# One level of Strassen's scheme for the up projection of a gated MLP, over pairs of a gate tile and a value tile, with the activations kept in DRAM

## Chip, cores, metric

One core of a Trainium2 chip runs one decoder layer. The metric is the device time of one execution in microseconds (us), from several runs; lower is better. PE is the tensor engine, DVE the vector engine, ACT the scalar engine, POOL is GpSimd, and SP is the engine that issues most DMAs.

## The reference

A decoder layer on 1024 tokens of width 1024 in float32: a Mamba-2 SSD branch and a latent attention branch, merged by gates and projected (`w_o`), then a gated MLP with a causal convolution over three tokens. Only the end is touched by the change:

```python
x = x + (g_ssd * y_ssd + g_mla * y_mla) @ w_o[i]
h = rms_norm(x, norm_ffn_g[i])
u = causal_depthwise_conv(h @ w_up[i], conv_ffn_w[i], conv_ffn_b[i])   # 1024 -> 2 * 2816
u_gate, u_val = jnp.split(u, 2, axis=-1)
x = x + (jax.nn.silu(u_gate) * u_val) @ w_down[i]                      # 2816 -> 1024
```

## The kernel before

Every large product is made of float32 numbers split in two: a rounded high part (type fp32r) and the rest. `split` (L126) makes the high part by a cast on ACT (L127) and the low part by a subtraction on DVE or POOL (L128). `mm3` (L147) multiplies two such numbers in three matmuls (L149 high by high, L150, L151 the cross terms), so one step over 128 input channels, for 128 output channels and 512 tokens, is three matmuls of 128x512.

The program is written in the order of the work. PE keeps the order in which the code is written. A scheduler may shift instructions on the other engines, each of which then takes its own in order; SP issues DMAs in order too, and one that has to wait holds up those behind it.

The stages at the end, with their places in the span: the SSD projection and merge for the two token halves, the output projection `w_o`, in the page's names `wops`, the norm (L208 to L229), transposition of the normed tokens to channels (`transposed`, L235 to L238), then the up projection and the down projection. `h2[half][k]` are the eight transposed and split tiles of a token half, in the pool `hp` (name `h`). The up projection goes over 22 gate tiles (kind 0) and 22 value tiles (kind 1) of 128 channels. For each it loads and splits the weight tile (`load_w`, names `wraw`, `whi`, `wlo`; the low part on DVE here), does eight steps of `mm3` for each half, and evacuates:

```python
ps = lin_tile()
yield from steps([w], h2[half], ps, range(KD), KD)
a = half * 512
S.copy(raw[:, 2 + a:2 + a + 512], ps)
c = act[:, a:a + 512] if kind == 0 else lt.tile([P, 512], F32, name="lt")
S.activation(c, ps, AF.Identity, bias=col(CG_FB + ct), scale=col(cw + 2))
for k in range(2):
    V.scalar_tensor_tensor(c, raw[:, a + k:a + k + 512], col(cw + k), c, op0=ALU.mult, op1=ALU.add)
if kind == 0:
    S.activation(c, c, AF.Silu)
else:
    V.tensor_tensor(act[:, a:a + 512], act[:, a:a + 512], c, op=ALU.mult)
```

The 22 tiles `act` (128 channels by 1024 tokens) stay in SBUF. The down projection goes over two halves of the output columns (`ch`) and 11 pairs of channel tiles (`kp`); it splits `act` again for each `ch` and accumulates into eight PSUM banks (six `dps`, two `lin`).

Of the kernel before, what the change touches and what calls it, by code (L numbers as in the profile page):

```python
# [9 lines left out]
F32 = mybir.dt.float32  # L10
# [7 lines left out]
P = 128  # L18
# [12 lines left out]
# column offsets of the packed per-partition parameters  # L31
# [19 lines left out]
# shape-only constants kept on chip; the rope tables and the attention mask follow them  # L51
# [5 lines left out]
# linear steps laid between the steps of the dependent chains, one digit for each place  # L57
# [15 lines left out]
def tile_hybrid_layer(ctx: ExitStack, tc: tile.TileContext, x, cols, cons, w_main, w_small, w_uq, w_ukv,  # L73
# [39 lines left out]
    def rsqrt_mean(dst, ss, n):  # L113
        # the halved exponent as a first guess, three Newton steps
# [32 lines left out]
    def mm3(ps, a, b, first, last):  # L147
        (ah, al), (bh, bl) = a, b
        PE.matmul(ps, lhsT=ah, rhs=bh, start=first, stop=False)  # L149
        PE.matmul(ps, lhsT=ah, rhs=bl, start=False, stop=False)  # L150
        PE.matmul(ps, lhsT=al, rhs=bh, start=False, stop=last)  # L151
# [25 lines left out]
    # linears that fill the tensor engine between the steps of the dependent chains  # L177
# [24 lines left out]
    def norm(tiles, outs, pool, ss=None, junk=None, group=1):  # L202
        """token-major rms norm; yields where other work may come in between"""
# [48 lines left out]
    # ---------------------------------------------------------------- linears of the hidden state that can wait  # L252
# [32 lines left out]
    # ---------------------------------------------------------------- norm, transposed hidden, token-major projection  # L285
# [44 lines left out]
        # the tensor engine's clock rises with its use: transposes of the identity until the data are there  # L330
# [43 lines left out]
    # q_a / kv_a norms and transposes  # L374
# [27 lines left out]
    # rope tables with the gains: [cos g1, sin g2, sin g1, cos g2]  # L402
# [7 lines left out]
    # shared rotary key part: sum of squares, rotated with gains  # L410
# [12 lines left out]
    # dt = softplus(raw + bias) = max(v, 0) + log1p(exp(-|v|)); log1p(e) = 2 atanh(e / (2 + e))  # L423
# [18 lines left out]
    # a = dt * -exp(a_log), its cumulative sums per chunk, the decays  # L442
# [15 lines left out]
    # the convolved channels come doubled: dt / 2 for x, dt / 8 for x, B and the C that reads the state  # L458
# [13 lines left out]
    # ---------------------------------------------------------------- attention  # L472
    with tc.tile_pool(name="cp", bufs=2) as cp, tc.tile_pool(name="pss", bufs=4, space=PSUM) as pss, \
# [3 lines left out]
        # the same mask with the keys on the partitions, and the negated identity  # L477
# [4 lines left out]
        # the columns of maxima stand last behind others, so that their row comes out in the place of the last channel  # L482
# [6 lines left out]
        def qkv_steps(pr):  # L489
            """q, k, v of a pair of heads, token-major, a half of the tokens at a time, with the norms and the rope"""  # L490
# [7 lines left out]
            for half in range(2):  # L498
                # a last channel: 0 of q, for the row of maxima, and 1 of k
# [64 lines left out]
        def maxima(pr, half, hd):  # L564
            """the greatest product of the high parts for each query of a half, negated, as a last row of q"""
# [28 lines left out]
        def key_block(pr, half, j, hd, accs):  # L594
            """exponentials of the scores of a key block for the queries of a half, transposed; their sums over blocks"""
# [24 lines left out]
        def output(pr, half, accs, pv):  # L620
            """values not yet normalized, and the sums as rows"""
# [30 lines left out]
        # the side steps of the units: done before the first key block, then after each step of the key blocks  # L652
        SIDE = [[1, 1, 1, 1, 1, 1, 1, 1, 2, 2, 2, 2], [1] * 10 + [0] * 1 + [2] * 7 + [0] * 6]

        def attention():
            """per unit (pair, half of the queries): key blocks one by one, the values two behind; the maxima of the
            next unit and the projection of the next pair go in between"""
# [14 lines left out]
            for pr in range(npair):  # L672
                for half in range(2):
# [13 lines left out]
                    # the first half's keys are overwritten only after their last use  # L687
# [28 lines left out]
    # ---------------------------------------------------------------- SSD, one group of eight heads at a time  # L716
    ya0 = [None] * 16
    head = []
    with tc.tile_pool(name="dp", bufs=2) as dp, tc.tile_pool(name="psx", bufs=1, space=PSUM) as psx, \
# [46 lines left out]
            # masked scores, transposed, with the decays  # L766
# [73 lines left out]
        def ssd_finish(g):  # L840
            # gate with silu(z) (kept doubled), then the group's norm
# [47 lines left out]
        def normalize(k):  # L889
            """attention output of two heads over its sums"""  # L890
# [61 lines left out]
    # ---------------------------------------------------------------- SSD branch projection, merge, output projection  # L952
    uctx = ExitStack()
    up = uctx.enter_context(tc.tile_pool(name="up", bufs=2))
    with tc.tile_pool(name="ep", bufs=2) as ep, tc.tile_pool(name="psw", bufs=4, space=PSUM) as psw, \
            tc.tile_pool(name="eps", bufs=2, space=PSUM) as eps_:
        x2h = []
        h2 = [[], []]
        for half in range(2):
            s = hs_(half)  # L960
            ya = ya0 if half == 0 else [load_act(y_d, k * P, s) for k in range(16)]
            ms = []
            for ct in range(8):
                gt = ep.tile([P, 512], F32, name="gt")
                nc.scalar.dma_start(out=gt, in_=g_d[ct * P:(ct + 1) * P, s])
                mt = ep.tile([P, 512], F32, name="mt")
                nc.scalar.dma_start(out=mt, in_=m_d[ct * P:(ct + 1) * P, s])
                if half == 0 and ct == 0:
                    ps = head[0]
                else:  # L970
                    ps = lin_tile()
                    drain([steps([load_w(w_ssd[ct, kp], [P, KD, P]) for kp in range(2)], ya, ps, range(16), 16)])
                V.scalar_tensor_tensor(gt, gt, 1.0, ps, op0=ALU.add, op1=ALU.mult)
                V.tensor_tensor(gt, gt, mt, op=ALU.add)
                m = ep.tile([P, 2, 512], F32R, name="m", bufs=8)
                S.mul(m[:, 0, :], gt, 0.5)
                V.scalar_tensor_tensor(m[:, 1, :], gt, 0.5, m[:, 0, :].bitcast(F32), op0=ALU.mult, op1=ALU.subtract)
                ms.append(m)
            if half:
                drain([norm(x2h[0], x2h[0], ep, x2ss)])  # L980
            x2s = []
            for i in range(4):
                t_ = ep.tile([P, D], F32, name="x2", bufs=8)
                r0 = (half * 4 + i) * P
                nc.sync.dma_start(out=t_, in_=x[r0:r0 + P, :])
                x2s.append(t_)
            x2h.append(x2s)
            sq4 = ep.tile([P, 4, 4], F32, name="sq4")
            for cq in range(4):
                banks = [psw.tile([P, 512], F32, name="wops") for _ in range(4)]  # L990
                qs = slice(cq * 256, (cq + 1) * 256)
                for kp in range(2):
# [179 lines left out]
```

## Time and profile before

| | us |
|---|---|
| runs | 2411.93, 2413.11, 2416.68 |
| median | 2413.11 |
| span of the profiled execution, first to last instruction | 2408.0 |
| PE busy in the span | 2277.5 (95%) |
| DVE, ACT, POOL busy | 1338.8, 1015.2, 489.5 |
| up projection, in the span | about 1684 to 2164.4 |
| down projection | 2164.4 to 2404 |

The profile gives the profiled execution its span and no time of its own; the median of the runs is 5.1 us over that span, which is what lies around it. Matmuls overlap in the pipe, so a matmul's duration in the profile (389 ns for 128x512) is not what it costs in a row of them; that is the distance between starts. In the whole up and down projection POOL does 44 small memsets and nothing else.

### The profile page before, as it was taken

The page shows a single profiled execution, that of the slowest core. Times are in us where ns is not written, and L with a number is a line of the kernel's source. Part 1 is how long each engine was busy: PE and PEld are TensorE (multiplying, and loading weights), DVE is VectorE, ACT ScalarE, POOL GpSimd, SP SyncE. Part 2 cuts the span into 40 slices and gives each one's busy share as a digit, 9 for nine tenths or more (in the row PEclk, how much of TensorE's full clock was granted, in tenths as well). Part 3 has the DMA queues.
Part 4 walks back from the last instruction along what each step waited for, and adds up shares of the span by engine and source line. Part 5 has one row for each costly group of instructions (what it writes and reads, how often), then busy time and mean ns, then how long its engine had stood idle before and what let it go on. Part 6 is the DMA issues. An engine that isn't in the chain of part 4 may idle for free.

```text
span 2408.0 us, 31951 instructions
## 1 busy us (share of the span) xinstructions
PE 2277.5 (95%) x11752; PEld 1833.4 (76%) x11752; DVE 1338.8 (56%) x2614; ACT 1015.2 (42%) x2020; POOL 489.5 (20%) x643
## 2 busy tenths in 40 slices
PE   8999999999999979988889699999999999999999
PEld 7877777777777757767667578989888888888887
DVE  4566666567644766767755555545544444453332
ACT  4454545444434364463643423424433333342221
POOL 2244443334423423232333300000000000000000
PEclk9999999999999989999999899999999999999999
DMA  3111111111126532243436466543111111111312
GB/s 134 54 63 59 50 46 36 59 50 50 40 69 183 158 90 76 91 108 91 90 124 221 145 225 203 171 149 116 61 44 53 44 53 44 53 44 61 104 63 87
DMA packets 139004, 220.57 MB, mean 92 GB/s; under 512 B 12544, under 2 KB 49088, under 8 KB 138848
## 3 DMA queue, kind: packets, MB, share of 16 engines
q1 hardware_dynamic: 133808, 208.97, 28.3%
q10 hardware_dynamic: 5040, 9.57, 1.1%
q8 instruction: 92, 1.51, 0.3%
q14 instruction: 64, 0.52, 0.1%
HBM read 173.14 MB, written 45.35 MB: 91 GB/s over the span
## 4 chain that ended last, share of the span: by engine, by line
PE 48%; DMA 9%; DVE 5%; ACT 3%; issue 3%; POOL 1%; SPq 0%; POOLq 0%; DVEq 0%; ACTq 0%
PE lin L149 11%; PE lin L150 11%; PE lin L151 11%; DMA abc<-ac_d 5%; PE dps L150 2%; PE dps L151 2%; PE dps L149 2%; DVE chan L740 2%; PE wops L151 1%; PE wops L150 1%; PE wops L149 1%; DMA zt<-z_d 1%; ACT seg L771 1%; PE yp L812 1%; DVE seg L774 1%
## 5 line engine op out<-in xcount | busy, mean ns | idle before, releaser
L149 PE MATMUL lin<-h,whi 128*128 128x512 f32 x1984 | 806.8, 407 | 29.3 <-ACT chan L738 19.1
L150 PE MATMUL lin<-h,whi 128*128 128x512 f32 x1984 | 782.1, 394 | 3.2 <-DVE h L128 3.2
L151 PE MATMUL lin<-h,wlo 128*128 128x512 f32 x1984 | 780.9, 394 | 2.1 <-DVE wlo L128 2.0
L149 PEld LDWEIGHTS lin<-h,whi 128*128 128x128 f32 x1984 | 378.3, 191 | 155.2 <-issue 54.4
L151 PEld LDWEIGHTS lin<-h,wlo 128*128 128x128 f32 x1984 | 377.2, 190 | 85.2 <-DVE wlo L128 2.9
L150 PEld LDWEIGHTS lin<-h,whi 128*128 128x128 f32 x1984 | 378.9, 191 | 72.6 <-DVE h L128 4.7
L127 ACT CAST whi<-wraw 128x512 fp32r<-128x512 f32 x372 | 223.9, 617 | 370.2 <-PE lin L150 151.7
L128 DVE TENSOR_TENSOR wlo<-wraw,whi 128x512 fp32r<-128x512 f32 x234 | 160.0, 695 | 221.5 <-ACT whi L127 218.7
L128 POOL TENSOR_TENSOR wlo<-wraw,whi 128x512 fp32r<-128x512 f32 x138 | 195.4, 1429 | 311.4 <-ACT whi L127 301.9
L606 ACT ACTIVATE e<-s 128x512 f32<-128x512 f32 (+1 forms) x192 | 93.4, 492 | 160.2 <-DVE s L604 109.4
L740 DVE SCALAR_TENSOR_TENSOR chan<-craw,cl,chan 128x512 f32<-128x512 f32 x144 | 143.8, 999 | 26.8 <-ACT chan L738 17.0
L1024 POOL MEMSET uraw<- 128x2 f32 x44 | 4.3, 100 | 746.0 <-DVE act L1036 495.9
L771 ACT ACTIVATE seg<-abc,acum 128x128 f32<-128x128 f32 x256 | 80.0, 389 | 134.9 <-DMA abc<-ac_d 125.0
L611 POOL TENSOR_TENSOR acc<-acc,e 128x512 f32<-128x512 f32 (+3 forms) x80 | 79.1, 989 | 222.6 <-ACT acc L609 134.4
L128 DVE TENSOR_TENSOR h<-act,h 128x1024 fp32r<-128x1024 f32 x44 | 53.1, 1224 | 104.2 <-ACT h L127 104.2
L1036 DVE SCALAR_TENSOR_TENSOR lt<-uraw,cl,lt 128x512 f32<-128x512 f32 x88 | 66.0, 750 | 75.3 <-ACT lt L1034 74.6
L149 PE MATMUL dps<-whi,h 128*128 128x512 f32 x264 | 102.7, 389 | 0.0
L150 PE MATMUL dps<-wlo,h 128*128 128x512 f32 x264 | 102.7, 389 | 0.0
L151 PE MATMUL dps<-whi,h 128*128 128x512 f32 x264 | 102.7, 389 | 0.0
L1036 DVE SCALAR_TENSOR_TENSOR act<-uraw,cl,act 128x512 f32<-128x512 f32 x88 | 66.0, 750 | 63.9 <-ACT act L1034 63.1
L127 ACT CAST h<-act 128x1024 fp32r<-128x1024 f32 x44 | 45.6, 1048 | 119.0 <-PE lin L150 112.9
L1032 ACT COPY uraw<-lin 128x512 f32<-128x512 f32 x88 | 51.5, 586 | 100.1 <-PE lin L151 100.0
(414 smaller groups left out, 3825.5 us busy)
## 6 DMA issues: line engine op xcount, KB each, us to landing
wraw<-in_w_main SPq DMA_DIRECT2D x112, 256.0 KB
wraw<-in_w_up SPq DMA_DIRECT2D x88, 256.0 KB
abc<-ac_d SPq DMA_DIRECT2D x32, 512.0 KB
wraw<-in_w_ssd SPq DMA_DIRECT2D x64, 256.0 KB
wraw<-in_w_down SPq DMA_DIRECT2D x44, 256.0 KB
g_d<-lt SPq DMA_DIRECT2D x32, 256.0 KB
z_d<-lt SPq DMA_DIRECT2D x32, 256.0 KB
zt<-z_d SPq DMA_DIRECT2D x32, 256.0 KB
```

Of the source, the lines that this page charges most:

```text
L127: S.copy(hi, raw)
L128: (eng or V).tensor_sub(lo, raw, hi.bitcast(F32))
L149: PE.matmul(ps, lhsT=ah, rhs=bh, start=first, stop=False)
L150: PE.matmul(ps, lhsT=ah, rhs=bl, start=False, stop=False)
L151: PE.matmul(ps, lhsT=al, rhs=bh, start=False, stop=last)
L606: S.activation(e[:, c0:512], ps[:, 0:w], AF.Exp)
L611: (V if hd else G).tensor_tensor(accs[hd][:, c0:512], accs[hd][:, c0:512], e[:, c0:512], op=ALU.add)
L740: V.scalar_tensor_tensor(c[:, s], raw[:, a + k:a + k + 512], col(cw + k), c[:, s], op0=ALU.mult, op1=ALU.add)
L771: S.activation(seg[:, hd, :], abc[:, hd, :], AF.Relu, bias=acum[:, c, 8 * g + hd:8 * g + hd + 1], scale=-1.0)
L774: V.tensor_tensor(seg, seg, sm.unsqueeze(1).broadcast_to([P, 8, P]), op=ALU.mult)
L1032: S.copy(raw[:, 2 + a:2 + a + 512], ps)
L1036: V.scalar_tensor_tensor(c, raw[:, a + k:a + k + 512], col(cw + k), c, op0=ALU.mult, op1=ALU.add)
```

## The change

The up projection of one gate tile and one value tile is taken as a product of a 2 by 2 matrix of weight blocks (rows: gate, value; columns: the two halves of the 1024 input channels) with a 2 by 2 matrix of activation blocks (rows: halves of the input channels; columns: token halves). It is computed with seven block products in place of eight, in the variant with shared sums. A block product is four steps of `mm3`.

- Activations: the seven blocks `11`, `21`, `22`, `t1` to `t4` (28 tiles `BQ[name][i]` of 128x512, split in two) are made once at the entry of the MLP from the transposed tiles. `h2_raw` transposes and scales without a split; DVE (L1192, L1203, L1210) and POOL (L1201) make the differences; `quarter` (L988 cast on ACT, L989 subtraction on DVE or POOL) splits.
- Weights: per pair `w_raw` loads the gate tile to `ur1` and the value tile to `ur2`, whole; `w_sums` makes sums and differences in four POOL instructions (L1100 to L1103); `w_first` to `w_fourth` split four sets (casts L1091, subtractions L1092; the first two sets on POOL, the others on DVE).
- The seven products are `p12` (two), `p5`, `p6`, `p7`, `p3`, `p4`; some accumulate onto an earlier one in its PSUM bank after that has been read. PSUM is read by ACT copies (L1134, L1144) and DVE additions (L1135, L1146, L1153, L1166, L1172) that put the parts together to `ug` and `uv` (1024 tokens). The convolution, SiLU and product then run on 1024 tokens at once (L1159 to L1174).
- The product is written to the DRAM tensor `a_d`; the down projection reads it back as `ar`, once for each `ch`.
- `x2_d` is written in pieces of 256 columns during `w_o`; all PSUM outside `lin` is one pool of six banks (`bank6`). The rows read at the end of the down projection have places of their own (`xr`).

The comments were also taken out of the code. The core of the diff:

```diff
+        def w_sums(q):
+            q.s = up.tile([P, KD, P], F32, name="us", bufs=1)
+            G.tensor_tensor(q.s[:, 0:4, :], q.r2[:, 0:4, :], q.r2[:, 4:8, :], op=ALU.add)
+            G.tensor_tensor(q.s[:, 4:8, :], q.s[:, 0:4, :], q.r1[:, 0:4, :], op=ALU.subtract)
+            G.tensor_tensor(q.r2[:, 0:4, :], q.r1[:, 0:4, :], q.r2[:, 0:4, :], op=ALU.subtract)
+            G.tensor_tensor(q.r1[:, 4:8, :], q.r1[:, 4:8, :], q.s[:, 4:8, :], op=ALU.subtract)
+        def w_second(q):
+            q.b = w_split(q.s, w_tiles(1), G)
+        def w_third(q):
+            q.c = w_split(q.r2, w_tiles(2), V)
...
+        def p5(q):
+            q.z = bank6()
+            drain([product(q.z, q.b, 0, "t1", True, True)])
+        def p6(q):
+            drain([product(q.x, q.b, 4, "t2", False, True)])
+            q.s2 = lt.tile([P, 512], F32, name="lt")
+            S.copy(q.s2, q.x)
+            q.q = lt.tile([P, 512], F32, name="lt")
+            V.tensor_tensor(q.q, q.z, q.s2, op=ALU.add)
+        def p7(q):
+            q.y = bank6()
+            drain([product(q.y, q.c, 0, "t3", True, True)])
...
+            V.tensor_tensor(q.uv[:, 514:1026], q.y, q.q, op=ALU.add)
...
+        def p3(q):
+            drain([product(q.z, q.d, 0, "22", False, True)])
+            V.tensor_tensor(q.ug[:, 514:1026], q.z, q.s2, op=ALU.add)
+            q.gate = conv(q, 0, q.ug)
+            S.activation(q.gate, q.gate, AF.Silu)
+        def p4(q):
+            drain([product(q.y, q.c, 4, "t4", False, True)])
+            V.tensor_tensor(q.uv[:, 2:514], q.y, q.s2, op=ALU.add)
+            c = conv(q, 1, q.uv)
+            V.tensor_tensor(q.gate, q.gate, c, op=ALU.mult)
+            nc.sync.dma_start(out=a_d[q.j * P:(q.j + 1) * P, :], in_=q.gate)
...
-        for j in range(2, FFT):
-            for kind in range(2):
-                drain([up_half(j, kind, 0), up_half(j, kind, 1)])
...
+    for j in range(3, FFT + 1):
+        nx = None
+        if j < FFT:
+            nx = Pair()
+            nx.j = j
+            w_raw(nx)
+            w_first(nx)
+            gate_row(nx)
+        p5(q)
+        if nx:
+            w_sums(nx)
+        p6(q)
+        if nx:
+            w_second(nx)
+        p7(q)
+        p3(q)
+        if nx:
+            w_fourth(nx)
+        p4(q)
+        if nx:
+            w_third(nx)
+            drain([p12(nx)])
+            c11(nx)
+        q = nx
...
+                    ar = fp.tile([P, T], F32, name="ar")
+                    nc.sync.dma_start(out=ar, in_=a_d[k * P:(k + 1) * P, :])
                     hi = hp.tile([P, T], F32R, name="h")
                     lo = hp.tile([P, T], F32R, name="h")
-                    split(acts[k], hi, lo)
+                    split(ar, hi, lo)
```

How instructions stand on the engines, at three places. In the names, a number after the last underscore is the buffer. First POOL, from the end of the SSD stage: before, the sums of squares of the last group's norm are followed by the memsets of the up projection alone.

```order
L858 TENSOR_TENSOR sqs<-sqs,sq__12696 128x512
L858 TENSOR_TENSOR sqs<-sqs,sq__12702 128x512
L858 TENSOR_TENSOR sqs<-sqs,sq__12708 128x512
L1024 MEMSET uraw 128x2 x44
```

Now, at the entry of the MLP, POOL splits pair 0's second set (`wlo_15698`), makes pair 1's sums and splits its second set, and does the quarters of the activations (`tq`, `h`) and the differences L1201, one after the other:

```order
L1092 TENSOR_TENSOR wlo_15698<-us_15692,whi_15697 128x1024
L1100 TENSOR_TENSOR us_15773<-ur2_15572 128x512
L1101 TENSOR_TENSOR us_15773<-us_15773,ur1_15571 128x512
L1102 TENSOR_TENSOR ur2_15572<-ur1_15571,ur2_15572 128x512
L1103 TENSOR_TENSOR ur1_15571<-ur1_15571,us_15773 128x512
L989 TENSOR_TENSOR tq_15660<-x2_13592,tq_15660 128x512
L1092 TENSOR_TENSOR wlo_15779<-us_15773,whi_15778 128x1024
L989 TENSOR_TENSOR tq_15689<-x2_13592,tq_15689 128x512
```

Four L1201 and six more L989 follow; the fifth of these six is the last that `p6` of pair 0 needs. Second, DVE in the middle of the up projection. Before, per weight tile (value tile, then the next gate tile):

```order
L1036 SCALAR_TENSOR_TENSOR lt_17220<-uraw_17182,cl_80,lt_17220 128x512 x2
L1040 TENSOR_TENSOR act_17109<-act_17109,lt_17220 128x512
L128 TENSOR_TENSOR wlo_17332<-wraw_17333,whi_17331 128x512
L1036 SCALAR_TENSOR_TENSOR lt_17251<-uraw_17182,cl_80,lt_17251 128x512
L128 TENSOR_TENSOR wlo_17332<-wraw_17337,whi_17331 128x512
L1036 SCALAR_TENSOR_TENSOR lt_17251<-uraw_17182,cl_80,lt_17251 128x512
```

Now, per pair:

```order
L1146 TENSOR_TENSOR lt_17316<-dps_17284,lt_17314 128x512
L1153 TENSOR_TENSOR uv_17335<-dps_17322,lt_17316 128x512
L1166 TENSOR_TENSOR ug_17144<-dps_17284,lt_17314 128x512
L1092 TENSOR_TENSOR xlo3_17357<-ur1_17274,xhi3_17356 128x512
L1161 SCALAR_TENSOR_TENSOR uc0_17351<-ug_17144,cl_80,uc0_17351 128x1024
L1172 TENSOR_TENSOR uv_17335<-dps_17322,lt_17314 128x512
L1161 SCALAR_TENSOR_TENSOR uc0_17351<-ug_17144,cl_80,uc0_17351 128x1024
L1092 TENSOR_TENSOR xlo2_17380<-ur2_17275,xhi2_17379 128x1024
L1161 SCALAR_TENSOR_TENSOR uc1_17373<-uv_17335,cl_80,uc1_17373 128x1024 x2
L1135 TENSOR_TENSOR ug_17282<-dps_17384,lt_17409 128x512
L1174 TENSOR_TENSOR uc0_17351<-uc0_17351,uc1_17373 128x1024
```

Five of the twelve read PSUM; the others read SBUF alone. POOL beside them does, per pair, L1100 to L1102, two memsets, a split L1092 of 128x1024, L1103 and another L1092. On ACT the cast of the next pair's second set stands ahead of the copy L1144 after `p6`. Third, SP at the border from up to down. Before, the weights of the down projection follow those of the up projection:

```order
L134 DMA wraw<-in_w_up 128x512 x84
L134 DMA wraw<-in_w_down 128x512 x16
L1062 DMA h<-x_d 128x512 x4
L134 DMA wraw<-in_w_down 128x512 x2
```

Now the first reads of the activations stand behind the write of the last pair, and the first of them waits for that write to have landed:

```order
L1175 DMA a_d<-uc_18455 128x1024
L1175 DMA a_d<-uc_18593 128x1024
L134 DMA wraw<-in_w_down 128x512 x4
L1175 DMA a_d<-uc_18712 128x1024
L1273 DMA ar<-a_d 128x1024 x12
L134 DMA wraw<-in_w_down 128x512 x2
L1273 DMA ar<-a_d 128x1024 x5
```

More of the change, by code (lines that the diff above doesn't have):

```diff
@@ L145, in load_w, with mm3 @@
         return hi, lo
[L147 removed]
+    def mm3(ps, a, b, first, last, **more):
         (ah, al), (bh, bl) = a, b
[L149 to L151 removed]
+        PE.matmul(ps, lhsT=ah, rhs=bh, start=first, stop=False, **more)
+        PE.matmul(ps, lhsT=ah, rhs=bl, start=False, stop=False, **more)
+        PE.matmul(ps, lhsT=al, rhs=bh, start=False, stop=last, **more)
     def act_tile():
@@ L1054, in tile_hybrid_layer @@
+    upctx.close()
+    tpctx.close()
+    with tc.tile_pool(name="fp", bufs=6) as fp:
         for ch in range(2):
-            banks = [psd.tile([P, 512], F32, name="dps") if t < 6 else lin_tile() for t in range(NT)]
+            banks = [bank6() if t < 6 else lin_tile() for t in range(NT)]
             xrs = []
```

287 lines of the change are left out of this document (199 added, 88 removed).

## Prediction

> **What bounds the kernel now.** I read busy time by stages first, then the groups of the up projection.
>
> ```profile
> span 2408.0 us, 31951 instructions
> 1700.00:2164.40 464.40, 464.40 (x2050) 384.56 (x2049) 214.64 (x306) 184.68 (x305) 4.20 (x42) 1.00 0.16 49
> 2164.40:2404.00 239.60, 239.60 (x1058) 198.21 (x1057) 85.31 (x100) 62.96 (x82) 0.00 (x0) 1.00 0.24 77
> ```
>
> Columns: stage and length, then busy us (instructions) of PE, weight loads, DVE, ACT and POOL, PE's granted clock, DMA share, GB/s. PE never rests in the up projection (first row), at full clock; DVE is busy for 46%, ACT for 40%, POOL for 1%. So PE's instructions set the time: 464.4 / 2050 = 0.2265 us for each matmul of 128x512, the price of a matmul removed here. PE waits for nothing.
>
> ```profile
> L150 PE MATMUL lin<-h,whi 128*128 128x512 f32 x683 | 265.7, 389 | 0.0
> L1036 DVE SCALAR_TENSOR_TENSOR act<-uraw,cl,act 128x512 f32<-128x512 f32 x86 | 64.5, 750 | 63.8 <-ACT act L1034 63.1
> L128 DVE TENSOR_TENSOR wlo<-wraw,whi 128x512 fp32r<-128x512 f32 x86 | 59.3, 689 | 109.2 <-ACT whi L127 109.2
> L127 ACT CAST whi<-wraw 128x512 fp32r<-128x512 f32 x86 | 53.2, 618 | 116.4 <-issue 78.2 <-PE lin L150 36.3 <-PE lin L151 1.9
> L1032 ACT COPY uraw<-lin 128x512 f32<-128x512 f32 x85 | 49.8, 585 | 95.2 <-PE lin L151 95.1
> L127 ACT CAST h<-act 128x1024 fp32r<-128x1024 f32 x44 | 45.6, 1048 | 119.0 <-PE lin L150 112.9 <-DMA out<-h 6.1
> L128 DVE TENSOR_TENSOR h<-act,h 128x1024 fp32r<-128x1024 f32 x44 | 53.1, 1224 | 104.2 <-ACT h L127 104.2
> L128 POOL TENSOR_TENSOR wlo<-wraw,whi x138: 1267/1296/2252, 38.5 to 1378.7; 128x512 fp32r<-128x512 f32 x138
> ```
>
> These give the prices (mean ns after the first bar; in the last row least, median and greatest, so 1.30 us for POOL). PE's 389 ns is pipelined and no price. For 128x1024: DVE subtraction 1.22, ACT cast 1.05, convolution step 0.75 + 0.53 (what 512 more elements add, 1.22 less 0.69) = 1.28.
>
> **Matmuls.** Eight products of 12 matmuls become seven: 22 x 12 = 264 fewer, and the order of PE shows 264 fewer of 128x512. Gain 264 x 0.2265 = 59.8 us. A pair takes 84 x 0.2265 = 19.0 instead of 21.7 us, a product 2.72.
>
> **Do the other engines keep up with 19.0 us a pair?** In this stage POOL did not work beside DVE before (4.2 us, memsets). What that does is seen earlier in the trace.
>
> ```profile
> 744.62 2.40 POOL L896 TENSOR_TENSOR nat<-nat,rb 128x1024 f32<-128x1024 f32 x1 [8.03 <-PE lin L151]
> 744.84 0.69 DVE L280 SCALAR_TENSOR_TENSOR lt<-lt,lin 128x512 f32<-128x512 f32 x1 [5.12 <-ACT lt L279]
> ...
> 757.12 2.40 POOL L896 TENSOR_TENSOR nat<-nat,rb 128x1024 f32<-128x1024 f32 x1 [7.61 <-DMA rb<-l_d]
> 757.17 2.89 DVE L740 SCALAR_TENSOR_TENSOR chan<-craw,cl,chan 128x512 f32<-128x512 f32 x1
> 759.48 1.74 POOL L128 TENSOR_TENSOR wlo<-wraw,whi 128x512 fp32r<-128x512 f32 x1
> 760.10 1.66 DVE L740 SCALAR_TENSOR_TENSOR chan<-craw,cl,chan 128x512 f32<-128x512 f32 x1
> 761.17 1.75 POOL L128 TENSOR_TENSOR wlo<-wraw,whi 128x512 fp32r<-128x512 f32 x1
> ...
> L740 DVE SCALAR_TENSOR_TENSOR chan<-craw,cl,chan x144: 739/752/2893, 750.7 to 1231.5; 128x512 f32<-128x512 f32 x144
> ```
>
> Start, length, engine. L740 reads two SBUF tiles and takes 0.752 at the median; started behind a POOL instruction it took 2.89, until that had ended, and then the two alternate: one DVE and one POOL instruction of 512 elements every 1.69 us (759.48 to 761.17). L280, with one input in PSUM, took its 0.69 beside POOL unharmed. So DVE's two-SBUF instructions and POOL's take turns.
>
> Per pair, in units of 512 elements: DVE has 13 such units (two splits 3, four convolution steps 8, product 2), POOL 8 (L1100 to L1103, two splits of 2). Eight turns of 1.69 and five DVE units of about 0.6 are 16.5 us; by full lengths (8.25 + 10.0) it is 18.3. Both are under 19.0. DVE's five PSUM additions (0.69 each) fit beside POOL; ACT has 8.2 us (three casts 1.05, one 0.62, two copies 0.59, two scalings about 1.1, SiLU 1.05). The tightest place is p3, which may write only when L1146 has read its bank: behind the end of p6 stand the cast 1.05, the copy L1144 0.59 and L1146 0.69 = 2.3, and p7 covers 2.72 less some 0.3 until p6's end is seen. It just fits, with 0.1 to spare. Laid out on from there, DVE's product ends at 15 us without turns; L1092 waits 0.9 and the product 2.1 for POOL, so 18, while the next L1146 is wanted at 20.7. I take 0.05 us of stall a pair, 1 us in 19 pairs; bounds 0 and 26 (below).
>
> Weights: the loads of pair q+2 leave when `ur2` of pair q has been split, a period before POOL wants them; their bytes do not grow. SP's queue holds nothing else there but `a_d`.
>
> **Entry.** Between the norm's end and p6 of pair 0 POOL must do 18 units (four sums, four L1201, eight quarters, a split of 2), DVE 24 (four each of L1192, L1203, L1210, twelve quarters). In turns: 18 x 1.69 + 6 x 0.6 = 34 us. PE has for that time 32 transposes (a quarter of a matmul each, 1.8), eight steps of 0.68, one product and the two p5: 15.4 us. So it waits 18.6, and 3 more for copy, cast and split of the third set behind p6. If there were no turns POOL's 18 x 1.3 alone would count: 23.4 - 15.4 = 8. About 4 of the 34 (pair 1's sums) can run during the norm. I take 17.5, near the turns, since the rows at 757 show them whole; ends 8 and 22.
>
> A gap has a second price.
>
> ```profile
> 1364.77 0.39 PE L817 MATMUL yp<-abc,st 128*64 128x128 f32 x4
> 1364.99 0.39 PE L812 MATMUL yp<-seg,xdt 128*64 128x128 f32 x4
> ...
> 1381.18 0.70 PE L812 MATMUL yp<-seg,xdt 128*64 128x128 f32 x4 [7.00 <-DVE seg L774]
> 1382.70 0.64 PE L812 MATMUL yp<-seg,xdt 128*64 128x128 f32 x4
> 1383.13 0.64 PE L817 MATMUL yp<-abc,st 128*64 128x128 f32 x4
> ...
> 1386.43 0.40 PE L151 MATMUL lin<-h,wlo 128*128 128x512 f32 x1
> 1380.00:1385.00 5.00, 3.48 (x30) 3.11 (x32) 4.06 (x5) 1.64 (x3) 0.00 (x0) 0.50 0.54 176
> ```
>
> After 7 us of rest the granted clock is 0.50 and groups of four stand 0.43 apart, not 0.22, until 1386.4: 5.2 us at half speed, 2.6 lost. I add 2.5 here: entry 20. The Trainium skill's page "TensorE: Matmul & The Clock Gate" (Part 1, What's actually happening) gives about 3.4 us of sustained work before the full clock; that would be an estimated 1.7 lost for each restart, and the sum 1.7 us better for the two. The trace has it longer, at 5.2, and stands.
>
> Pair 1's third set is split between pair 0's convolution steps, so p7 waits about 1 us once.
>
> **Border to the down projection.** Before, PE goes over without a gap, `act` being on chip. Now, after the last p4, stand L1172 0.69, a gate step 1.28, two value steps 2.56, the product 1.22 and 0.3 to see p4's end: 6.0. Then the write and the read.
>
> ```profile
> 822.59 3.26 DMA at_d<-nat
> 1405.01 3.58 DMA lt<-y_d
> 1425.00:1560.00 135.00, 130.69 (x758) 114.77 (x757) 70.17 (x159) 49.02 (x102) 0.13 (x2) 1.00 0.62 205
> ```
>
> A write of 512 KB and a read of 256 KB take 3.3 and 3.6 us in the chain of waits; the read here stands behind the write. 6.0 + 3.3 + 3.6 + cast 1.05 + split 1.22 = 15.1, all on the path, since PE has nothing else in its order; with the restart 2.6 it is 17.7. Ends: 11.8 (no wait for the write, no cold clock) and 20 (512 KB read slower). After that a pair of tiles (10.9 us of PE) needs 1.5 MB, 144 GB/s; the stage at 1425 moved 205 with PE 97% busy. Hidden, at 0; so are the x2 writes during `w_o` (24 DMAs more, in SP's waits for weights already split ahead) and the transposes' banks there (six before, six now).
>
> **Sum.** -59.8 + 1 + 20 + 1 + 17.7 = -20.1 us, on a span of 2408.0; the median of the runs is 5.1 higher, 2413.1. So 2393 us, 0.8% faster. What a measurement can tell from no change is about 0.2%, 4.8 us.
>
> **Rivals.** (1) DVE and POOL do not only alternate but starve the chain: if DVE, strictly in order, stands still whenever POOL works, a pair takes DVE's 11.0 (its 13 units at 0.6, five PSUM additions at 0.65) and POOL's 9.3 (its own part of a turn, 1.16 from 760.06 to 761.22 four times and 2.35 from 757.17 to 759.52 twice) = 20.3 us, 1.35 x 19 = 26 us more: 2419, slower. It decides from 20.1 us a pair on. For it: the 2.89 above. Against it: five DVE instructions don't meet POOL, and the product waits for nobody within 2.6 us. The Trainium skill's page "SBUF — State Buffer" (Who interferes with whom) says that the second of two such instructions fully blocks, while a DVE instruction with one SBUF input does not contend; the trace agrees, 2.89 against 0.69. (2) The seams cost little: no turns at the entry (8), read not behind the write (12): -59.8 + 1 + 8 + 1 + 12 = -38, 2375. Against it the rows at 757 and SP's order. (3) Reading `ar` starves PE: at 100 GB/s a pair of tiles needs 15.7 us, 4.8 x 22 = 106 us more, 2499; the row with 205 GB/s speaks against it. (4) The entry longer still: 22 in place of 17.5, DVE's norm behind one split on POOL (2.35), and PE at half speed for all five products of pair 0 after it (13.6, of which 2.5 is counted): 18 us more, 2411, no change. For it the clock row; against it that 5.2 us of work brought the clock back.
>
> **Numbers.** Forecast (PE paces the pairs, both seams cost; 2381 to 2406) 0.60; (2) 0.15; (1) 0.14; (3) 0.02; (4) 0.09. Faster 0.75, same 0.09, slower 0.16. The range takes in (2) and, upward, (4) and a pair at 20.1 us nearly reached: 2375 to 2416.
>
> **What would show it.** Right: between the third pair and the last, PE without gaps, pairs 19.0 us apart; POOL some 9 us a pair and DVE lengths of 2 to 3 us in single instructions; a gap of 15 to 22 us in pieces before pair 0's p7, and one of about 15 just before the first `dps` matmul with `ar` behind it, each followed by a clock of 0.5. Wrong: pairs over 20 us, with PE waiting for L1146 or for `wlo`; PE waiting for `ar` in the down projection; an entry that PE's order covers.

## The result

The changed kernel takes 2433.7 us (median, 2430.7 to 2437.8) and the kernel before, run on the same chip, 2414.9 (2411.9 to 2420.4): ratio 1.0082, 95% interval 1.0062 to 1.0102. It is slower by some 19 us where 20 less were forecast, a miss of about 40. The profiled execution took 2430.7, its span is 2428.9.

To place the loss, both traces are cut at the same points of the program. The columns are those of the prediction's first rows. First the kernel before: SSD projection of the second half (from 1548), its output projection (1635), up projection (1682), down projection (2165).

```profile
1547.69:1634.76 87.07, 87.07 (x387) 72.11 (x385) 40.90 (x94) 23.96 (x44) 0.00 (x0) 1.00 0.46 151
1634.76:1682.33 47.57, 47.57 (x417) 47.57 (x416) 25.39 (x57) 21.39 (x53) 0.00 (x0) 1.00 0.30 96
1682.33:2164.67 482.34, 482.34 (x2146) 399.76 (x2145) 230.50 (x362) 195.82 (x325) 4.20 (x42) 1.00 0.16 52
2164.67:2408.00 243.33, 239.52 (x1057) 198.01 (x1055) 85.73 (x101) 62.96 (x82) 0.00 (x0) 1.00 0.24 78
```

Then the changed kernel, its up projection in three: the entry (pairs 0 to 3), pairs 4 to 21, and the border.

```profile
1552.27:1660.50 108.23, 96.33 (x388) 74.98 (x387) 51.76 (x111) 33.81 (x60) 0.00 (x0) 0.94 0.47 148
1660.50:1708.07 47.57, 47.57 (x417) 47.57 (x416) 24.17 (x45) 21.83 (x55) 11.22 (x8) 1.00 0.39 128
1708.07:1821.53 113.46, 93.52 (x370) 71.69 (x369) 85.48 (x91) 50.45 (x69) 69.20 (x46) 0.86 0.19 63
1821.53:2168.86 347.33, 347.33 (x1513) 283.91 (x1511) 247.21 (x220) 147.86 (x163) 184.72 (x133) 1.00 0.24 79
2168.86:2183.00 14.14, 0.14 (x2) 0.14 (x1) 6.28 (x7) 3.31 (x4) 0.00 (x0) 0.67 0.35 132
2183.00:2428.90 245.90, 241.79 (x1056) 199.27 (x1056) 88.86 (x100) 66.25 (x83) 0.00 (x0) 0.99 0.48 164
```

The differences of these rows:

| stage | forecast | measured |
|---|---|---|
| all ahead of 1547.7 / 1552.3 | 0 | +4.6 (in the kernels below it ends anywhere from 1548 to 1557) |
| SSD projection of the second half | 0 | **+21.2** |
| output projection of the second half | 0 | 0.0 |
| up projection without its border | -37.8 | **-21.6** |
| border, PE idle | +15.1 | +14.1 |
| down projection | +2.6 | +2.6 |
| sum | -20.1 | +20.9 |

Half of the miss lies ahead of the up projection, where the prediction has no cost. There PE waits for the high parts of y (first row, of PE's waits from 1552 to 1661: total, times, longest), since SP issues all 16 of their loads (L158) from 1554 us on, behind the last x2 writes (the second and third lines, of SP's queue):

```profile
PE lin L149 <- ACT h L127: 9.8, 4, 6.1
1549.33 4.91 SPq L1040 DMA_DIRECT2D x_d<-x  x4
1554.28 1.39 SPq L158 DMA_DIRECT2D lt<-y_d  x3
```

The stage's 21.2 us are 11.9 of idle PE (108.23 - 96.33) and 9.3 more of busy time for the same matmuls, at a granted clock of 0.94. In the kernel before 13 loads are issued between 1494.91 and 1517.7, beside the loads of `w_o` (three went earlier):

```profile
1494.91 2.13 SPq L158 DMA_DIRECT2D lt<-y_d  x3
...
1511.79 5.95 SPq L158 DMA_DIRECT2D lt<-y_d  x4
```

### The profile page after: what moved, and what is told of

The parts are those of the page before. It is cut to its first block, busy times and chain, and to the rows that moved or that the text cites. A ratio compares the mean times of both kernels' runs of the same rounds, so it can differ in the third digit from the quotient of the medians.

```text
span 2428.9 us, 31637 instructions
## 1 busy us (share of the span) xinstructions
PE 2246.8 (93%) x11488; PEld 1790.3 (74%) x11488; DVE 1452.3 (60%) x2556; ACT 1025.7 (42%) x1933; POOL 755.5 (31%) x792
## 4 chain that ended last, share of the span: by engine, by line
PE 40%; DMA 12%; DVE 7%; ACT 4%; issue 3%; POOL 1%; SPq 0%; POOLq 0%; ACTq 0%; DVEq 0%
PE dps L151 7%; PE dps L149 7%; PE dps L150 7%; PE lin L150 5%; PE lin L149 5%; PE lin L151 5%; DMA abc<-ac_d 5%; DVE chan L740 2%; DMA zt<-z_d 1%; ACT seg L771 1%; DMA wraw<-in_w_ssd 1%; DMA lt<-y_d 1%; DMA rb<-l_d 1%; POOL wlo L128 1%; DMA wraw<-in_w_mla 1%
## 5 line engine op out<-in xcount | busy, mean ns | idle before, releaser
L149 PE MATMUL lin<-h,whi 128*128 128x512 f32 x1448 | 601.1, 415 | 43.0 <-ACT chan L738 18.2
L150 PE MATMUL lin<-h,whi 128*128 128x512 f32 x1448 | 577.9, 399 | 9.2 <-DVE h L128 5.1
L151 PE MATMUL lin<-h,wlo 128*128 128x512 f32 x1448 | 575.2, 397 | 3.7 <-DVE wlo L128 2.2
L149 PEld LDWEIGHTS lin<-h,whi 128*128 128x128 f32 x1448 | 278.7, 192 | 154.2 <-issue 56.0
L151 PEld LDWEIGHTS lin<-h,wlo 128*128 128x128 f32 x1448 | 278.0, 192 | 67.1 <-DVE wlo L128 3.9
L150 PEld LDWEIGHTS lin<-h,whi 128*128 128x128 f32 x1448 | 279.1, 193 | 63.4 <-DVE h L128 10.1
L127 ACT CAST whi<-wraw 128x512 fp32r<-128x512 f32 x288 | 172.3, 617 | 249.0 <-PE lin L150 101.6
L128 DVE TENSOR_TENSOR wlo<-wraw,whi 128x512 fp32r<-128x512 f32 x150 | 102.4, 702 | 110.3 <-ACT whi L127 110.1
L128 DVE TENSOR_TENSOR h<-ar,h 128x1024 fp32r<-128x1024 f32 x44 | 53.9, 1225 | 122.0 <-ACT h L127 121.5
L127 ACT CAST h<-ar 128x1024 fp32r<-128x1024 f32 x44 | 46.4, 1054 | 140.7 <-PE lin L150 129.4
L611 DVE TENSOR_TENSOR acc<-acc,e 128x512 f32<-128x512 f32 (+3 forms) x80 | 58.5, 731 | 49.4 <-ACT e L606 33.7
L617 PE MATMUL pv<-e,vt 128*64 128x512 f32 (+3 forms) x384 | 82.7, 511 | 0.0
L1091 ACT CAST xhi<-ur 128x1024 fp32r<-128x1024 f32 (+1 forms) x44 | 36.7, 836 | 107.8 <-PE dps L150 106.8
L989 POOL TENSOR_TENSOR h<-x,h 128x512 fp32r<-128x512 f32 x10 | 13.8, 1380 | 217.1 <-ACT h L988 217.1
```

Of the source, the lines that this page charges most:

```text
L127: S.copy(hi, raw)
L128: (eng or V).tensor_sub(lo, raw, hi.bitcast(F32))
L149: PE.matmul(ps, lhsT=ah, rhs=bh, start=first, stop=False, **more)
L150: PE.matmul(ps, lhsT=ah, rhs=bl, start=False, stop=False, **more)
L151: PE.matmul(ps, lhsT=al, rhs=bh, start=False, stop=last, **more)
L611: (V if hd else G).tensor_tensor(accs[hd][:, c0:512], accs[hd][:, c0:512], e[:, c0:512], op=ALU.add)
```

## The experiments

**1 to 3: why the loads of y come late.** One line of the change is not in the part of its diff shown above. In the output projection ACT squares each new piece of x2 for the norm's sum; the squares themselves are thrown away. Their place was a tile of its own (`junk`, 128x256); it now is a tile `lt`, one of the ring of three buffers through which `load_act` (L156) reads y. Buffers of a ring are given out in the order of the code, so the 16 squares of the first half come ahead of the 16 loads. In the changed kernel's chain of waits the last of these squares (ACT `lt` L1038) ends at 1554.28 us, and the first load of y leaves at 1554.28.

```diff
 # 1, from the changed kernel
-    junk = lt.tile([P, 512], F32, name="lt")[:, 0:256]
+    junk = em.tile([P, 256], F32, name="junk")
 # 2, from the kernel before
-    junk = ep.tile([P, 256], F32, name="junk")
+    junk = lt.tile([P, 512], F32, name="lt")[:, 0:256]
 # 3, from the changed kernel: ahead of the end of the half
-    nc.sync.dma_start(out=x2_d[r0:r0 + P, qs], in_=big[:, i, qs])      # 16 a half
+    nc.sync.dma_start(out=x2_d[r0:r0 + P, :], in_=big[:, i, :])        # 4 a half, at its end
```

> The changed kernel with one line put back: the squares of the output projection, whose values nobody reads, go to a tile of their own again (2 buffers of 128x256) and no longer to lt, the ring of 3 buffers through which the rows of y_d are loaded. Theory A (ring): the 16 squares of the first half of the tokens stand in that ring ahead of the 16 loads of y_d for the second half, so the loads cannot start before the last squares; with the line put back they start near 1500 us as before, PE's 9.8 us of waits for h from ACT L127 fall under 2 us, the half-speed clock around 1560 to 1580 goes, and the time falls by 17 to 21 us, from 2433.7 to 2413 to 2417. Theory B (queue): the loads are late because 16 short writes of x2 stand ahead of them in SP's queue; then they stay late, and the time stays within 4 us of 2433.7.

> The kernel before with that one line of the change alone: its squares go to lt. Nothing else is changed, its up projection is the old one. Theory A (ring): the kernel before loses what the changed kernel loses there, 17 to 21 us: 2432 to 2436, with the loads of y_d for the second half after 1545 us. Theory B: no difference, 2411 to 2418.

> The changed kernel with x2 written as before, in whole rows of 1024 columns, 4 writes behind each half, where it now writes 16 pieces of 256 columns from within the half; the squares stay in lt. Theory A (ring): no gain, 2430 to 2437, loads of y_d still after 1545 us. Theory B (queue of short writes): 17 to 21 us less, 2413 to 2417.

Measured: 1 took 2414.6 us, ratio to the kernel before 1.0000 (0.9982 to 1.0018). 2 took 2435.9, ratio 1.0084 (1.0061 to 1.0108). 3 took 2428.0, ratio 1.0054 (1.0037 to 1.0071). The same stage in the three, in this order, then the issue of the loads of y in the first and the third:

```profile
1548.20:1635.39 87.19, 87.19 (x387) 72.23 (x386) 41.31 (x95) 24.31 (x44) 0.00 (x0) 1.00 0.43 136
1552.86:1661.12 108.26, 95.77 (x386) 74.33 (x385) 51.51 (x110) 33.64 (x60) 0.00 (x0) 0.94 0.49 160
1553.34:1660.63 107.29, 95.52 (x386) 73.93 (x385) 51.62 (x111) 33.81 (x60) 0.00 (x0) 0.94 0.51 162
1495.37 2.12 SPq L158 DMA_DIRECT2D lt<-y_d  x3
1554.72 2.40 SPq L158 DMA_DIRECT2D lt<-y_d  x3
```

The one line makes the loss (108.3 in a kernel with the old up projection) and its return takes it away (87.2, no wait). The form of the x2 writes has nothing to do with it: the loads stay at 1554 us and the stage at 107.3. Kernel 3's 5.7 us below the changed kernel are outside both expectations; its trace shows 1 us of them in this stage and none in the up projection, and its profiled execution as a whole is no shorter (span 2429.2 against 2428.9). No trace shows where they come from, so they stay open.

**4: the border.** The last pair has no next weights to load, so `ur1` and `ur2` are free, and the tiles `h` of the first operand too.

```diff
+    if nx is None:                                   # last pair, ahead of p5
+        for k in range(4):
+            t = up.tile([P, KD, P], F32, name=f"ur{1 + k % 2}", bufs=2)...
+            nc.sync.dma_start(out=t, in_=a_d[k * P:(k + 1) * P, :])
+            early.append((t, hp.tile(...), hp.tile(...)))
     ...
     p7(q)
+    for e in early: split(*e)
     p3(q)
     ...
+    if ch == 0 and k < 4: pair.append(early[k][1:]); continue
```

> The changed kernel, with the first four rows of tiles of the activations (pairs 0 to 3) read back and split during the last pair, into the buffers ur1 and ur2, which have no weights left to take, and into tiles h that the last pair no longer needs. Down's first pass reads them from there. If the 14 us in which PE waits at the border come from the last product's chain, its write and the first read back, as the prediction says, they go, and with them the 2.5 us of the clock's restart: 2417 to 2420. Rival: the loads of rows 4 and 5 wait for the same buffers and the gap only moves to them, 21 us later: a gap of 5 us or more there, and a gain under 6 us.

Measured: 2413.7, ratio 0.9994 (0.9977 to 1.0010), 20 us below the changed kernel and 3 below the forecast range; the traces show 15.9 of the 20 at the border and behind it. The border of the changed kernel in the chain of waits, then PE at the border and the two stages of this kernel (up projection with its border, down projection):

```profile
2174.02 1.24 DVE uc L1174
2175.27 2.60 DMA a_d<-uc
...
2178.07 3.60 DMA ar<-a_d
...
2181.77 1.05 ACT h L127
2168.78 0.40 PE L151 MATMUL dps<-tq,xlo 128*128 128x512 f32 x1
2169.01 0.39 PE L149 MATMUL dps<-whi,h 128*128 128x512 f32 x1
1707.23:2169.01 461.78, 440.72 (x1882) 355.86 (x1881) 334.54 (x314) 201.69 (x236) 253.40 (x179) 0.97 0.23 79
2169.01:2412.10 243.09, 239.53 (x1057) 198.07 (x1055) 90.37 (x102) 65.17 (x82) 0.00 (x0) 1.00 0.49 167
```

The border was the chain that the prediction laid out (product 1.24, write 2.60, read 3.60, cast 1.05), less the split of 1.22: PE's first matmul needs the high part alone and starts at 2182.86, 0.04 us behind the cast. With four rows read early PE goes over 0.23 us after its last matmul, up and border are 13.1 us shorter and down 2.8 (no restart). The wait did not move to row 4, and reading the activations from DRAM in both passes costs nothing: 243.1 against 243.3 before.

**5: both.** 

> The changed kernel with both edits that worked alone: the squares in a tile of their own, and the first four rows of activations read back and split during the last pair. The two losses lie in stages 600 us apart, so they should add up: the stage between the two halves of the output projection as in the kernel before (87 us from 108), the border without a wait (461.9 us from the end of the output projection to down, as with the early rows alone). In the traces that is 21 plus 15.4 us off 2433.7: 2394 to 2402, faster than before. Rival: with the one gone the other shrinks to what the noise of the stages ahead allows; 2405 or more.

Measured: 2396.2, ratio 0.9930 (0.9913 to 0.9947). The two gains add up: the SSD stage takes 87.1 us, and from the end of the output projection to down 462.9.

**6, 7 and 9: the entry.** What PE waits for from 1708 to 1821 us in the changed kernel (first seven rows: total, times, longest), and a piece of what POOL and DVE do just then:

```profile
PE lin L149 <- ACT h L988: 5.3, 3, 2.4
PE dps L149 <- DVE lt L1146: 3.8, 1, 3.8
PE dps L151 <- DVE xlo L1092: 3.2, 1, 3.2
PE lin L150 <- DVE h L989: 2.8, 2, 2.5
PE dps L976 <- DVE x L229: 2.0, 1, 2.0
PE dps L149 <- ACT xhi L1091: 1.6, 1, 1.6
PE lin L150 <- POOL h L989: 1.1, 2, 0.6
1732.01 5.94 POOL L1201 TENSOR_TENSOR x<-x 128x512 f32<-128x512 f32 x4
1733.32 1.77 DVE L1203 TENSOR_TENSOR x<-x,x 128x512 f32<-128x512 f32 x1 [2.44 <-POOL x L1201]
```

DVE's 512 elements take 1.77 us beside POOL, behind a wait of 2.44 for it. Three kernels, each from the changed one:

```diff
 # 6: GpSimd's work of the entry on VectorE (w_sums of pair 1, w_second of pairs 0 and 1, b3, low parts)
-    G.tensor_tensor(b[3, i], b[4, i], b[3, i], op=ALU.subtract)
+    V.tensor_tensor(b[3, i], b[4, i], b[3, i], op=ALU.subtract)
-    quarter("t2", i, b[4, i], act_tile(), G if i % 2 else V)           # t1, t3, t4 likewise
+    quarter("t2", i, b[4, i], act_tile(), V)
 # 7: ahead of each step of pair 0's p6 (n = 11, 14, 14, 17), and 7 ahead of its p7
+    for _ in range(n):
+        PE.matmul(q.y, lhsT=q.b[0][:, 0, :], rhs=BQ["11"][0][:, 0, :], start=True, stop=True)
 # 9: the first of 6's edits alone (b3)
```

> The changed kernel, with all that GpSimd computes between the norm of the second half and pair 0's third product put on VectorE: the differences b3, the low parts of t1 to t4, the second weights of pairs 0 and 1 and the sums of pair 1 (16 operations of 512 and 6 of 512 to 1024). Theory T (turns, as in the prediction): two engines in turns of 1.7 us a pair of operations do less than VectorE alone at 0.60 us each; 42 operations in 25 us where they took 34, the t2 tiles come 6 to 10 us earlier, PE's waits from 1737 to 1757 us (12 us) fall under 6, and the time falls by 6 to 12 us, to 2422 to 2428. Theory W (VectorE is the bound and GpSimd a help): VectorE gets 40% more operations, the t2 tiles come later, and the time rises by 3 to 10 us.

> The changed kernel with 63 matmuls added that compute nothing that is used (into the bank that pair 0's third product overwrites): 11, 14, 14 and 17 ahead of the four steps of pair 0's second product, and 7 ahead of its third, so that PE is busy where it waits now. They cannot bring the operands earlier. Theory C (clock): of the 33 us that the entry costs above its matmuls about 20 are waits and 13 are matmuls at half clock, which each short wait sets back; with PE kept busy the clock stays at 1.0 from 1737 to 1757 us and the time falls by 5 to 9 us, to 2425 to 2429. Theory D (operands): the low clock is hidden in the waits, since PE is early anyway; same time within 3 us, or longer by what the added matmuls overrun.

> The changed kernel with the four differences b3 alone on VectorE; all else of the entry stays on GpSimd. It parts two reasons why the entry got shorter without GpSimd. Theory Q (queue): the first step of each t2 tile overwrites what b3 still has to read, and b3 stands in GpSimd's queue behind the sums and the second weights of pair 1 (VectorE waited 2.4 us for it at 1733 us); then these four operations give most of it, and the stage from the end of the output projection to down falls from 474.9 by 6 us or more. Theory T (turns): it is the sharing itself, so 4 of GpSimd's 22 operations give 4/22 of 10.8 us: 2 us, 472 to 474.

Measured: 6 took 2414.0, ratio 1.0003 (0.9991 to 1.0015); 7 took 2423.7, ratio 1.0043 (1.0024 to 1.0062); 9 took 2431.3, ratio 1.0067 (1.0042 to 1.0091). The entry of 6 and of 7 (113.46 in the changed kernel), the up projection with its border of 9 (474.9 in the changed kernel), and DVE in the entry of 6:

```profile
1702.11:1804.70 102.59, 89.48 (x370) 70.76 (x369) 83.90 (x109) 50.05 (x69) 36.09 (x28) 0.92 0.21 70
1705.23:1814.50 109.27, 100.71 (x434) 81.15 (x433) 84.72 (x91) 50.39 (x70) 66.47 (x46) 0.95 0.19 66
1710.22:2183.72 473.50, 439.23 (x1882) 354.91 (x1880) 344.78 (x320) 201.01 (x235) 246.53 (x175) 0.97 0.23 77
1717.29 0.68 DVE L1201 TENSOR_TENSOR x<-x 128x512 f32<-128x512 f32 x1
1717.89 0.68 DVE L989 TENSOR_TENSOR tq<-x,tq 128x512 fp32r<-128x512 f32 x1
```

How far the entry scatters is seen in kernels 1, 3, 4 and 5, where it is unchanged: 115.9, 113.7, 114.6 and 115.8 us, with DVE busy for 83.1 to 87.4. The changed kernel's 113.46 is the shortest of the five.

Without POOL, DVE starts one such instruction every 0.60 us (1717.29 to 1717.89), has 18 instructions more and is busy for no more time, 83.9 us; the entry is 10.9 us shorter, clear of that scatter. So it is the turns: a helper that makes a DVE instruction of 0.68 us take 1.77 takes away more than it does. This is the exclusive turn that the Trainium skill's page "SBUF — State Buffer" (Who interferes with whom) states, and the trace agrees (1.77 us beside POOL, 0.68 without). It is not one place in POOL's queue, which should have given 6 us or more: b3 alone gives 1.4 us, which is within the scatter and no more than its share (4 of the 18 instructions moved, not of 22 as the expectations have it: 2.4). Of 6's 19.7 us the entry is 10.9; 6.0 more lie ahead of it in the trace, where nothing was changed, so that its time lies below the range of theory T for a reason that T does not have.

Keeping PE busy with 63 matmuls whose results nobody reads makes the entry *shorter*, by 4.2 us, the granted clock rising from 0.86 to 0.95. So the low clock does cost time there, at least 4.2 of the 13 us at stake, just below what theory C had (5 to 9) and more than theory D (3 at most). The time as a whole fell by 10.0, of which 2.8 lie ahead of the entry in the trace. Whether the rest of the 13 us is hidden beside other waits, as D has it, no run here shows.

**8, 10 and 11: the edits together, and the pairs.** 8 joins 5 and 6 and exchanges two tiles: in the changed kernel the products p7, p3 and p4 take their weights from tiles named x, p12, p5 and p6 from `whi` and `wlo`; in 8, from pair 2 on, p5 and p6 use x tiles and p7 and p4 `whi`. 10 is 8 with the loop's `w_first`, `w_sums` and `w_second`, and the last two of pair 2, on VectorE; 11 is 10 with `w_second` in the loop back on GpSimd.

```diff
 # 8, in w_tiles
-    if n < 2:
+    if n in ((0, 1) if ux[0] is None else (0, 2)):
 # 10
-    q.a = w_split(q.r1, w_tiles(0), G)
+    q.a = w_split(q.r1, w_tiles(0), V)
-    w_sums(nx)      w_second(nx)
+    w_sums(nx, V)   w_second(nx, V)
```

> Both edits of the kernel with ring and rows, GpSimd's work of the entry on VectorE, and an exchange: from pair 2 on the second set of weights lies in the upper buffers (xhi) and the third in the lower ones (whi). By theory T 6 to 12 us below the kernel with ring and rows alone: 2384 to 2394; by theory W above it. The exchange tells why 36 of a pair's 84 matmuls took 0.2331 us and not 0.2269: if it is where their weights lie, the third product and the last (weights now whi) come down to 0.227 and the fifth and sixth (now xhi) go up to 0.233; if it is which product it is, or what runs beside it, the third and last stay at 0.233. The time of a pair stays 19.3 us either way.

> The kernel with all three edits, and the pairs' own weight sums, first and second weights on VectorE as well, so that GpSimd does nothing in the up projection but two memsets a pair. At 0.60 us for 512 columns and 1.13 to 1.2 for 1024 VectorE has 10.7 us a pair now and gets 4.7 more: 15.4 of the pair's 19.3 us. If turns are what costs (theory T), nothing gets longer: pairs stay at 19.3 us, the product of gate and value falls from 2.7 to 1.2 us, and PE's waits for pairs 0 to 2 (14 us in all) shrink by 2 to 6 us: 2378 to 2382. Rival: VectorE in one queue answers PE later, and PE waits in every pair: a pair above 19.5 us, and the time above 2388.

> The kernel with the pairs' weight work on VectorE, with the low part of the second set, in the loop alone, back on GpSimd: on VectorE it stood right ahead of the sum of pair q (L1146) for which PE's third-quarter product waits. If that one place in the queue made a pair 19.67 us long instead of 19.32, pairs come back to 19.3, and the waits of pairs 0 to 2 stay as short as with all of it on VectorE: from the end of the output projection to down 442 to 446 us (447.2 and 454.2 in the two kernels before), in all 2377 to 2383. If it is the sum of VectorE's work in a pair (15.8 us busy), taking 1.2 us away gives back a quarter of it and pairs stay above 19.55.

Measured: 8 took 2383.5, ratio 0.9880 (0.9861 to 0.9899); 10 took 2388.3, ratio 0.9886 (0.9866 to 0.9906); 11 took 2381.2, ratio 0.9858 (0.9840 to 0.9877). All three beat the kernel before by over 1%; among themselves the intervals overlap, and the traces have to tell. First the exchange: 12 matmuls of p6 (`whi`) and p7 (x) in the changed kernel, then 24 of p5 and p6 (x) and 12 of p7 (`whi`) in 8.

```profile
1887.56:1890.28 2.72, 2.72 (x13) 2.25 (x12) 1.96 (x1) 0.00 (x0) 2.64 (x2) 1.00 0.01 2
1890.28:1893.08 2.80, 2.80 (x13) 2.26 (x12) 0.69 (x1) 1.53 (x2) 2.02 (x2) 1.00 0.46 187
...
1950.17:1955.76 5.59, 5.59 (x26) 4.52 (x25) 4.78 (x3) 1.05 (x1) 4.35 (x3) 1.00 0.23 89
1955.76:1958.49 2.73, 2.73 (x13) 2.25 (x12) 0.69 (x1) 1.53 (x2) 1.91 (x2) 1.00 0.47 192
```

2.80 and 5.59 / 2 against 2.72 and 2.73: the slower pace goes with the tiles, not with the product or its neighbours. For p4, also on `whi` in 8, this holds in part: it comes down from 2.80 only to 2.75.

Then the pairs. From the end of the output projection to down 8 needs 447.1 us, 10 needs 454.1 and 11 needs 452.1; pairs are 19.32, 19.67 and 19.56 us apart. In 10 PE's waits of over 0.3 us for pairs 0 to 2 did shrink, from 13.2 us in 8 to 10.2, but the entry got no shorter by it (99.4 us in 8, 100.5 in 10, at a granted clock of 0.95 and 0.92). And now PE waits in every pair, at p3:

```profile
1879.96 1.22 DVE L1092 TENSOR_TENSOR xlo<-us,xhi 128x1024 fp32r<-128x1024 f32 x1 [2.30 <-ACT xhi L1091]
1881.11 0.68 DVE L1146 TENSOR_TENSOR lt<-dps,lt 128x512 f32<-128x512 f32 x1
1881.37 0.39 PE L151 MATMUL dps<-tq,wlo 128*128 128x512 f32 x1
1881.85 0.50 PE L149 MATMUL dps<-h,xhi 128*128 128x512 f32 x1
```

L1146, which reads the bank that p3 writes next, ends at 1881.79 since a split of 1.2 us was ahead of it in DVE's queue; p3 starts at 1881.85, 0.48 behind p7's last matmul and not 0.23, and the first matmul behind the gap takes some 0.1 us longer: together the 0.35 by which a pair grew. In 11 the split is gone from there and p3 on time, but the same gap has moved to the next product: L1153, whose bank p4 writes, stands behind two of the sums, one of which waits for POOL.

```profile
1880.30 0.69 DVE L1100 TENSOR_TENSOR us<-ur 128x512 f32<-128x512 f32 x1 [1.32 <-POOL xlo L1092]
1881.64 0.68 DVE L1153 TENSOR_TENSOR uv<-dps,lt 128x512 f32<-128x512 f32 x1
1882.01 0.40 PE L151 MATMUL dps<-h,xlo 128*128 128x512 f32 x1
1882.38 0.51 PE L149 MATMUL dps<-tq,whi 128*128 128x512 f32 x1
```

So in 10 the rival came out (a pair above 19.5 us, the time just above 2388), by the order in DVE's queue. In 11 pairs stayed at 19.56, as its second reading has it; but the trace puts the gap behind one place in the queue again, and not behind the sum of VectorE's work. The turns do no harm in the pairs, where DVE has slack (kernel 8, with POOL at work, has no such gap); the place in the queue does.

## Why the prediction was wrong

- **Failed: nothing but "hidden, at 0" for the stages ahead of the up projection.** I priced the x2 writes and the transposes there, rightly at 0 (47.57 us before and after; experiment 3). I did not follow the tile that the squares moved to, and so had no term for it: 21.2 us, half of the miss. It is a line of no arithmetic and no instruction more; what it changes shows only in SP's order, where the loads of y moved behind the x2 writes.
- **Failed: the size of the entry's restart.** Entry and pair 1's third set were 21 us; measured are 33.4 (113.46 less 336 x 0.2265 = 76.1 and less the 3.9 that the stage before had beside its matmuls). The waits were nearly right in sum, 19.9 (113.46 - 93.52) for 18.5, but in part by luck: up to pair 0's p7 they are 12.9 for 17.5, with the turns among their causes (experiment 6), then 3.2 for the third set of pair 1, priced at 1, and 3.8 for L1146 in pair 2, for which there was no term. The clock was not: 2.5 for one restart, where the rest of the 33.4 is 13.5. The wait came in eleven pieces, and PE worked at half speed between most of them (granted clock 0.58 from 1737 to 1757 us). In the three stretches of the entry with a clock of 0.50 PE is busy for 18.9 us; half of that, 9.4, is an estimate of what it lost. That was rival 4's mechanism, at a chance of 0.09. Experiment 7 shows at least 4.2 of it as time that can be had back.
- **Half failed: "+1" for the pairs.** They came 19.30 us apart (347.33 / 18), 4.9 in all above 19.03. PE indeed has no gap between them, and neither turns nor L1146 take anything; it is the tiles of 36 of 84 matmuls, which the rows that I read of the kernel before do not show (experiment 8). The slack of 0.1 us at p3 was real: one split more ahead of L1146 uses it up (experiment 10).
- **Right:** the 264 matmuls at 0.2265 us; the border, 14.1 idle for 15.1, its pieces as laid out but for the split (1.22, not in the way) and the write (2.6 for 3.3), and 2.6 for the restart behind it; nothing for reading the activations in both passes of down.
- **The rivals.** (1) fell: pairs at 19.3, not 20.3, though POOL works 10 us in each. (2) had both seams cheap; both cost. (3) fell. (4) came nearest: one step of DVE's norm (L229) took 2.87 us behind POOL's split, and PE waited 2.0 for it (priced 2.35); half speed lasted beyond one restart (9.4 lost by the estimate above, priced 13.6); but its wait of 22 did not come. None had a loss ahead of the up projection.

With the line put back, four rows read early and POOL kept out of the entry, the scheme brings 30 us (2413.7 to 2383.5), half of the 59.8 that its matmuls save.

## To carry to other kernels

A scratch tile whose content nobody needs still takes a place in its ring: before moving one, list what else is allocated from that ring behind it, above all loads that are to run ahead. Read a change's effect on the DMA queue's order stage by stage, also where its arithmetic is not. Where the vector engine is the bound, giving GpSimd a share of two-input work in SBUF can make the whole slower; give it work where the vector engine has slack, and keep the reads that free a PSUM bank at the head of the queue.

## What was not expected of the hardware

Matmuls of one shape run at 0.2265 or at about 0.233 us by the tile that holds their weights (2.72 and 2.80 us for 12); which property of the tile decides, its place in SBUF or another, was not tried.

The clock fell at once behind a wait of 2.46 us in the changed kernel, and in kernel 8 only 1.4 us after one of 3.38 (the first matmul behind a wait is longer in any case). In both traces the record of the granted clock changes at steps that are multiples of 3.41 us (in the changed kernel at 1723.15, 1740.22, 1760.70 and 1774.35 us). Cut at these steps, the first stretch below is of the changed kernel and ends with the fall; the other three are of kernel 8. The two single lines are the matmuls behind the two waits.

```profile
1740.23 0.79 PE L150 MATMUL lin<-h,whi 128*128 128x512 f32 x1 [2.46 <-DVE h L989]
1736.81:1740.22 3.41, 0.95 (x5) 0.45 (x3) 3.41 (x3) 1.14 (x2) 2.71 (x2) 1.00 0.00 0
...
1745.53 0.50 PE L151 MATMUL dps<-tq,wlo 128*128 128x512 f32 x1 [3.38 <-DVE wlo L1092]
1740.15:1743.56 3.41, 2.01 (x9) 1.31 (x7) 3.41 (x3) 0.37 (x1) 1.32 (x1) 1.00 0.57 154
1743.56:1746.97 3.41, 1.44 (x6) 1.22 (x7) 3.37 (x4) 3.38 (x4) 0.10 (x1) 1.00 0.25 24
1746.97:1750.38 3.41, 3.41 (x9) 2.45 (x9) 3.41 (x5) 1.73 (x3) 1.38 (x2) 0.50 0.33 132
```

The shorter wait lies whole in one stretch, in which PE was busy for 0.95 us, and half speed followed. The longer one is cut in two: behind 2.01 us of work in a stretch the clock stayed, behind 1.44 it fell. Where the border between the two lies was not tried.

The Trainium skill's page "TensorE: Matmul & The Clock Gate" (Part 1, What's actually happening) says that the clock is set by activity over a free-running window of 3.4 us. That fits the stretches above; that one with 1.44 us of work was enough is more than the page's rule of one idle window says.
